# One down projection over all tokens, with seven products made of seven each, in a convolution and SwiGLU layer

## The chip, the cores and the metric

The kernel runs on one core of a Trainium2 chip. The metric is device time in microseconds. PE is TensorE, PEld its weight loads, DVE is VectorE, ACT is ScalarE, POOL is GpSimd and SP is SyncE; SP and ACT issue all DMAs here.

## What is computed

One layer (D = 1024, 2048 tokens, float32): a short gated convolution and a SwiGLU feed-forward, each between two RMS norms with shift, scale and gate that come from a conditioning vector `c`.

```python
mod = silu(c) @ ada_w + ada_b
sh_m, sc_m, g_m, sh_f, sc_f, g_f = split(mod, 6)
h = rms_norm(x, gain0) * (1 + sc_m) + sh_m
b, cc, v = split(h @ conv_w_in, 3)            # 1024 x 3072
h = (b * causal_conv3(cc * v)) @ conv_w_out   # 1024 x 1024
x = x + g_m * rms_norm(h, gain1)
h = rms_norm(x, gain2) * (1 + sc_f) + sh_f
g, u = split(h @ w_gate_up, 2)                # 1024 x 5632
h = (silu(g) * u) @ w_down                    # 2816 x 1024
out = x + g_f * rms_norm(h, gain3)
```

## The kernel before

**Tiling.** Features lie on the 128 partitions, tokens along the rows. The tokens go in two units (u = 0, 1) of 1024, each of two halves of 512 (tok = 0, 1; `CH` = 512). One matmul multiplies a 128 x 128 weight tile by a 128 x 512 tile of features.

**Three matmuls for a product.** Operands are split: `high` (or `upper`) is a cast on ScalarE to the type that TensorE takes in one pass (fp32r), `low` (or `lower`) is the rest, subtracted by VectorE. A product is high x high + low x high + high x low, so a slot of the schedule, four tiles of depth, is 12 matmuls.

**Seven products instead of eight.** Each matrix product of a unit is cut in two along tokens, depth and columns, and done by the Strassen-Winograd scheme with products P1 to P7. The sums of weight blocks and of feature blocks (A11, A12, A22, S1 to S4, see `FEATURES`) are made ahead, stored to HBM and loaded again. The products accumulate in PSUM or are added by VectorE on the way out (`Group.after`).

**Stages.** in0, out0, in1, out1, gu0, down0, gu1, down1 (in: first projection; out: `conv_w_out`; gu: gate and up; down: `w_down`). For a down stage `lockstep` gives an order of slots: seven products, each for four column groups, in three pieces of depth (`SUBS`: 4, 4 and 3 tiles of the 11). Between stages the first two slots of the next are put ahead of the last two of the one before.

**The order of the work is written out by hand.** The main loop walks the slots. `schedule(slot, f)` puts a piece of work at a slot, `later(n, f)` puts it n slots on, a generator's `yield n` waits n slots. Each engine does its instructions in the order of the program. `supply` keeps the weights ahead: loaded 9 slots before use (`BLOCKS`), `high` 5, `low` 4.

**Side work that the change touches.**
- `sums_later("down", ...)`: during gu0 POOL makes the weight sums of both down stages, SP loads the blocks, ACT stores the results.
- `add_square`: the squares of a finished tile (ACT) are added to a running sum, by POOL (`E=G`) except in parts of the last stage.
- `after_out`: norm after the convolution, residual, x1 to HBM, squares for the next norm. For unit 1 it runs in gu0.
- `normalized`: scales, shifts and splits the inputs of a stage at slots around its start; for gu1 this falls at the end of down0.
- `after_down`: norm of a finished half (`norm_of_sums`, `root` on POOL, `diagonal`, `spread`), then eight tiles of output. For unit 0 the halves are stored (`z2_d`) and finished during gu1.
- `last_half`: the last half of the last stage. Its x1 tiles are ready (`before_last`); the last tile's squares go to TensorE at once; output tiles are added on TensorE, POOL and VectorE (`ON_PE`, `ON_POOL`, `LAST_TURN`).

Pools: `raw` 16 tiles of 128 x 512, `big` 17 of 128 x 2048, `tmp` 10, PSUM 8 banks.

## Time and profile before

| | us |
|---|---|
| median of 3 runs (1958.24 to 1961.13) | 1959.97 |
| the profiled execution | 1961.33 |
| its span in the trace | 1959.5 |
| TensorE busy in the span | 1934.8 |
| VectorE busy | 1446.5 |
| ScalarE busy | 899.6 |
| POOL busy | 343.8 |

462.14 MB moved by DMA, 236 GB/s over the span. The granted TensorE clock was 0.998. In the profile L78 is the line of the helper that records every instruction, so groups are told apart by the names of their tiles: `down1P` is a PSUM bank of the stage down1 as well as, with numbers before the P (`down6P`), the weights of a product; `down1S`, `down1A` are features, `down1z` results, `down1q` squares, `o10` the norm of unit 1's first half. A number in the `x` column counts instructions; "idle before" is the engine's idle time just ahead of the group, with what ended it.

### The profile page before, as it was taken

What the parts mean: (1) busy time and instruction counts of PE and PEld (TensorE: products, weight loads), DVE (VectorE), ACT (ScalarE), POOL (GpSimd) and SP (SyncE); (2) the same over time, 40 slices, a digit from 0 to 9 for tenths busy, and PEclk for the clock granted to TensorE, in tenths of its full rate; (3) what the DMA queues carried; (4) which work ended last, traced back from release to release, by engine and by line L of the source; (5) the groups of instructions that cost most, each with busy time, mean ns of one, the idle gap of its engine ahead of it and who ended that gap; (6) DMA issues with size and microseconds to landing.
All of it is one profiled execution on the core that took longest, in us unless ns stands there. A gap on an engine that the chain in (4) does not pass through costs nothing.

```text
span 1959.5 us, 24903 instructions
## 1 busy us (share of the span) xinstructions
PE 1934.8 (99%) x8454; PEld 1570.0 (80%) x8454; DVE 1446.5 (74%) x2069; ACT 899.6 (46%) x1419; POOL 343.8 (18%) x226
## 2 busy tenths in 40 slices
PE   8899999999999999999999999999999999999998
PEld 4678887878878888888888888888888888888886
DVE  4898898977998776997776755587776655665466
ACT  4543457634446743543333454473333333444452
POOL 0012112211221301243341410120100100111011
PEclk9999999999999999999999999999999999999999
DMA  9369979769996764777665977588654332386534
GB/s 390 138 227 373 339 253 349 268 225 371 323 324 216 279 232 149 238 241 244 213 214 183 313 281 269 192 287 279 203 192 140 127 137 97 118 321 226 196 134 133
DMA packets 207632, 462.14 MB, mean 236 GB/s; under 512 B 24465, under 2 KB 39953, under 8 KB 201105
## 3 DMA queue, kind: packets, MB, share of 16 engines
q1 hardware_dynamic: 181584, 406.40, 60.1%
q10 hardware_dynamic: 25920, 54.16, 7.3%
q8 instruction: 66, 1.08, 0.2%
q14 instruction: 62, 0.50, 0.1%
HBM read 329.38 MB, written 131.09 MB: 235 GB/s over the span
## 4 chain that ended last, share of the span: by engine, by line
PE 80%; DVE 8%; DMA 6%; ACT 3%; issue 2%; SPq 0%; ACTq 0%; POOL 0%; DVEq 0%
PE gu1P L78 21%; PE gu0P L78 18%; PE in0P L78 11%; PE down0P L78 11%; PE down1P L78 11%; PE in1P L78 3%; PE out1P L78 2%; PE out0P L78 2%; DMA x<-xx 1%; PE pms L78 1%; DMA kgu1P<-gu1P 1%; DVE in1b L78 0%; DVE in1y L78 0%; DVE gu0a L78 0%; DMA xr<-x_d 0%
## 5 line engine op out<-in xcount | busy, mean ns | idle before, releaser
L78 DVE TENSOR_TENSOR gu1a<-gu1P,gu1a 128x512 f32<-128x512 f32 x63 | 43.5, 691 | 108.5 <-PE gu1P L78 108.5
L78 DVE TENSOR_TENSOR gu0a<-gu0P,gu0a 128x512 f32<-128x512 f32 x63 | 43.3, 688 | 71.7 <-PE gu0P L78 68.8
L78 POOL TENSOR_TENSOR gu1a<-gu1a 128x512 f32<-128x512 f32 x11 | 19.0, 1731 | 360.0 <-DVE gu1g11s L78 39.9
L78 ACT COPY gu1a<-gu1P 128x512 f32<-128x512 f32 x42 | 24.7, 589 | 96.1 <-PE gu1P L78 85.0
L78 POOL TENSOR_TENSOR nq<-nq,nq 128x512 f32<-128x512 f32 x28 | 42.8, 1529 | 136.1 <-ACT nq L78 131.4
L78 ACT COPY gu0a<-gu0P 128x512 f32<-128x512 f32 x42 | 24.4, 586 | 82.2 <-PE gu0P L78 81.0
L78 DVE CUSTOM_DVE_ANT_0 ada<-ada,c 128x512 f32<-128x512 f32 x80 | 60.1, 762 | 0.0
L78 ACT COPY gu1g<-gu1P 128x512 f32<-128x512 f32 x24 | 14.1, 588 | 92.8 <-PE gu1P L78 88.0
L78 POOL TENSOR_TENSOR gu0a<-gu0a 128x512 f32<-128x512 f32 x11 | 19.4, 1767 | 170.6 <-ACT gu0a L78 45.3
L78 ACT COPY gu0g<-gu0P 128x512 f32<-128x512 f32 x24 | 14.1, 589 | 74.4 <-PE gu0P L78 71.0
L78 POOL TENSOR_TENSOR down0q<-down0q,down0q 128x512 f32<-128x512 f32 x14 | 21.0, 1502 | 148.1 <-ACT down0q L78 148.1
L78 ACT ACTIVATE nq<-xx 128x512 f32<-128x512 f32 x32 | 37.1, 1159 | 17.0 <-DVE xx L78 17.0
L78 POOL TENSOR_TENSOR down1q<-down1q,down1q 128x512 f32<-128x512 f32 x10 | 16.1, 1612 | 148.6 <-ACT down1q L78 148.5
L78 DVE TENSOR_TENSOR gu1g<-gu1P,gu1g 128x512 f32<-128x512 f32 x24 | 16.6, 691 | 24.4 <-ACT gu1g L78 23.0
L78 DVE TENSOR_TENSOR down2P<-down2P,down2P 128x512 fp32r<-128x512 f32 x14 | 11.2, 801 | 29.0 <-ACT down2P L78 29.0
L78 ACT ACTIVATE gu1a<-gu1a 128x512 f32<-128x512 f32 x42 | 26.6, 633 | 13.1 <-DVE xo L78 6.0
L78 ACT ACTIVATE gu0a<-gu0a 128x512 f32<-128x512 f32 x42 | 26.6, 634 | 7.3 <-DVE gu0a L78 6.1
L78 POOL TENSOR_TENSOR out1q<-out1q,out1q 128x512 f32<-128x512 f32 x14 | 19.9, 1422 | 55.2 <-ACT out1q L78 55.1
L78 POOL TENSOR_TENSOR out0q<-out0q,out0q 128x512 f32<-128x512 f32 x14 | 20.8, 1485 | 46.9 <-ACT out0q L78 29.7
L78 DVE TENSOR_TENSOR gu0g<-gu0P,gu0g 128x512 f32<-128x512 f32 x24 | 16.5, 689 | 14.3 <-ACT gu0g L78 12.9
L78 DVE TENSOR_TENSOR xx<-xx,zz 128x512 f32<-128x512 f32 x32 | 25.1, 784 | 1.1
L78 ACT ACTIVATE down0q<-down0z 128x512 f32<-128x512 f32 x16 | 18.4, 1153 | 14.9 <-DVE down0z L78 14.8
(3139 smaller groups left out, 6715.8 us busy)
## 6 DMA issues: line engine op xcount, KB each, us to landing
ada<-ada_d SPq DMA_DIRECT2D x64, 256.0 KB, 5.3
act0A<-gu0a SPq DMA_DIRECT2D x33, 256.0 KB, 3.5
act1A<-gu1a SPq DMA_DIRECT2D x33, 256.0 KB, 2.6
ada<-ada_d SPq DMA_DIRECT2D x16, 512.0 KB, 9.5
zz<-z SPq DMA_DIRECT2D x32, 256.0 KB, 5.7
xx<-xt_d SPq DMA_DIRECT2D x32, 256.0 KB, 5.5
x<-xx ACTq DMA_DIRECT2D x32, 256.0 KB, 5.4
down0S<-act0S SPq DMA_DIRECT2D x8, 1024.0 KB, 7.3
```

Source lines behind the costliest of these rows:

```text
L78: return tc.keep_in_program_order(f(*args, **kwargs))
```

## The change

- The two down stages become one, `down0`, after gu1 and over all 2048 tokens. The outer seven products halve tokens within a unit (tok), depth and columns; each is made by seven inner products that halve units, ten of the eleven tiles of depth and the columns again. Tile 11 of the depth is added to four of the inner products (`PLAIN`). One inner product is three steps of 12, 12 and 6 or 12 matmuls.
- Weight sums are made in two passes (`outer_sums`, `inner_sums`) by VectorE during gu0 and the start of gu1; a second pass of feature sums (`feature_sums`, 35 jobs of four) by VectorE during gu1 and, for the last part, the down stage. All go through HBM: SP loads, ACT stores.
- Inner products are collected in eight tiles C11 to C22 by additions on VectorE (`evict`).
- `add_square` uses VectorE everywhere.
- Gu1 follows gu0 directly; its inputs are prepared at gu0's end, two slots later against the stage's start than before (`GU1_EARLY`). The last modulation (`mods_later((5,), ...)`) moves from down0 into gu1. The first product of the down stage is not interleaved with gu1's last slots.
- At the end two halves finish close together: (unit 1, tok 0) and (unit 0, tok 0). The output of the first is kept as eight pieces (`ph.tiles`); two are issued inside the wait times of the other's norm (`fill`), the rest behind its output.
- Small shifts in `normalized` (A11 in two parts, S4 one slot later); the weight sums of the out stages are stored two slots after the addition instead of three.

```diff
-SUBS = ((0, 4), (4, 4), (8, 3))
+KQ = FH // 2
+QW = KQ * 2 * P
+PARTS = ((0, 512), (512, 1024), (1024, QW))
...
+X_LOAD, X_HIGH, X_LOW = 6, 4, 3
+GU1_EARLY = 0
+INNER_AT = (8, 74, 89, 104, 119, 162, 186)
+INNER_EVERY = (9, 5, 5, 5, 5, 8, 8)
...
+OUTER_TURN = ("P1", "P6", "P7", "P4", "P5", "P2", "P3")
+INNER_TURN = ("P1", "P7", "P6", "P4", "P5", "P2", "P3")
+EARLY_TURN = ("P1", "P2", "P6", "P7", "P5", "P4", "P3")
+FIRST_OF = {"P1": "11", "P7": "22", "P6": "21", "P3": "12"}
+SECOND_OF = {"P2": "11", "P5": "22", "P4": "21"}
+LAST_OF = {"P2": "11", "P5": "22", "P4": "21", "P3": "12"}
+PLAIN = {"P2": 0, "P3": 0, "P7": 1, "P4": 1}
+RAW_BLOCK = {"P1": 0, "P2": 3, "P3": 2}
...
+    def block_sums(pace, E, load, n, store):
+        b11, b12 = load(0), load(1)
+        yield pace
+        b22 = load(2)
+        yield pace
+        E.tensor_tensor(b11[:, :n], b12[:, :n], b11[:, :n], ALU.subtract)
+        later(2, partial(store, "P5", b11))
+        b21 = load(3)
+        yield pace
+        E.tensor_tensor(b12[:, :n], b22[:, :n], b12[:, :n], ALU.subtract)
+        later(2, partial(store, "P7", b12))
+        yield pace
+        E.tensor_tensor(b22[:, :n], b22[:, :n], b11[:, :n], ALU.subtract)
+        later(2, partial(store, "P6", b22))
+        yield pace
+        E.tensor_tensor(b21[:, :n], b21[:, :n], b22[:, :n], ALU.subtract)
+        later(2, partial(store, "P4", b21))
+        yield pace
...
+    def outer_sums(pace, E):
+        for op in ("P5", "P7", "P6", "P4"):
+            outer_w[op] = [scratch([P, QW], f"kdown{op}{v}") for v in range(4)] + [scratch([P, CH], f"kdown{op}r")]
+        for v in range(5):
+            for c0, c1 in PARTS if v < 4 else ((0, CH),):
+                part = lambda t, c0=c0, c1=c1: t[:, c0:c1]
+                src = [w_down[b, v] if v < 4 else w_rest[b] for b in range(4)]
+                load = lambda b, src=src, part=part, v=v: from_hbm(part(src[b]), f"down{v}b{b}")
+                store = lambda op, t, part=part, v=v, n=c1 - c0: A.dma_start(part(outer_w[op][v]), t[:, :n])
+                yield from block_sums(pace, E, load, c1 - c0, store)
+    def inner_sums(op, c0, c1, pace, E):
+        src = outer_w[op]
+        load = lambda v: from_hbm(src[v][:, c0:c1], f"downq{op}{v}")
+        store = lambda o, t: A.dma_start(inner_w[op, o][:, c0:c1], t[:, : c1 - c0])
+        yield from block_sums(pace, E, load, c1 - c0, store)
...
+    def all_inner_sums(op, first, every, pace, E):
+        for o in ("P5", "P7", "P6", "P4"):
+            inner_w[op, o] = scratch([P, QW], f"qdown{op}{o}")
+        for n, (c0, c1) in enumerate(PARTS):
+            schedule(first + n * every, lambda c0=c0, c1=c1: run(inner_sums(op, c0, c1, pace, E)))
+        schedule(first + len(PARTS) * every - 1, lambda: run(inner_rest(op, E)))
+    def feature_sums(o, m, pace, lag, E):
+        def load(u, k):
+            t = raw(f"x{o}{u}{k}")
+            SP.dma_start(t, act_d[u][o][:, k, :])
+            return t
+        def store(i, t):
+            A.dma_start(inner_d[o][i][:, m, :], t)
+        x21, x22 = load(1, m), load(1, KQ + m)
+        yield pace
+        x11 = load(0, m)
+        yield pace
+        E.tensor_tensor(x22, x21, x22, ALU.add)
+        later(lag, partial(store, "S1", x22))
+        x12 = load(0, KQ + m)
+        yield pace
+        E.tensor_tensor(x21, x11, x21, ALU.subtract)
+        later(lag, partial(store, "S3", x21))
+        yield pace
+        E.tensor_tensor(x11, x22, x11, ALU.subtract)
+        later(lag, partial(store, "S2", x11))
+        yield pace
+        E.tensor_tensor(x12, x12, x11, ALU.subtract)
+        later(lag, partial(store, "S4", x12))
...
+            units = [(k, g) for k in range(KQ) for g in range(2)][4 * part : 4 * part + 4]
+            if part == 2 and i in PLAIN:
+                units += [(KQ, g) for g in range(2)]
+            self.units = units
...
+    def nested(ph):
+        return [Step(ph, op, i, part) for op in OUTER_TURN
+                for i in (EARLY_TURN if op == OUTER_TURN[0] else INNER_TURN) for part in range(len(PARTS))]
...
-    def add_square(acc, key, z, name, E=G, lag=1, in_turn=True):
+    def add_square(acc, key, z, name, E=V, lag=1, in_turn=True):
...
+            sums = any(op == "P1" and i in ("P5", "P6", "P7") and k == KQ - 1 for _, op, i, k in four)
+            ready = 2 if sums else -X_LOAD
+            schedule(first + max(n - X_LOAD, ready), load)
+            schedule(first + max(n - X_HIGH, ready + 1), upper)
+            schedule(first + max(n - X_LOW, ready + 2), lower)
...
-                                       ("gu", 0), ("down", 0), ("gu", 1), ("down", 1))]
+                                       ("gu", 0), ("gu", 1), ("down", 0))]
...
-        if slots and slots[-1].ph.kind in ("in", "gu"):
+        if slots and slots[-1].ph.kind in ("in", "gu") and not ph.last:
...
+        def tile(k, lag):
+            z = ph.z(u, tok, k)
+            V.tensor_tensor(z, z, rb[0], ALU.mult)
+            V.tensor_tensor(xt[k], xt[k], z, ALU.add)
+            later(lag, partial(A.dma_start, out_tile(u, tok, k), xt[k]))
+        if not tok:
+            load(0)
+            load(4)
+            yield 4.5
+            q = at_once(norm_of_sums(ph.acc[u, tok], f"o{u}{tok}"))
+            yield 1
+            dg = diagonal(q, f"o{u}{tok}")
+            yield 1
+            rb[0] = spread(dg, f"o{u}{tok}")
+            ph.tiles = [partial(tile, k, 0.5) for k in range(KD)]
+            return
+        yield 6
+        q = yield from norm_of_sums(ph.acc[u, tok], f"o{u}{tok}")
+        yield from spread_later(q, f"o{u}{tok}", partial(put, rb, 0), 3)
+        if not u:
+            yield 7
         load(0)
-        yield 1
         load(1)
         yield 2
         for k in range(KD):
             if k + 2 < KD:
                 load(k + 2)
-            z, xt = tiles.pop(k)
-            V.scalar_tensor_tensor(z, z, col(mG[1], k), rb[0], ALU.mult, ALU.mult)
-            V.tensor_tensor(xt, xt, z, ALU.add)
-            later(1, partial(A.dma_start, out_tile(u, tok, k), xt))
-            yield 1.5 if ph.last else 2
+            tile(k, 2.5)
+            yield 1.5
+    LAST = (0, 0)
...
+        def fill():
+            if ph.tiles:
+                ph.tiles.pop(0)()
...
+        fill()
         V.tensor_tensor(v, v, ph.st[:, :4], ALU.add)
-        q = at_once(root(v, "last"))
+        steps = root(v, "last")
+        next(steps)
+        fill()
+        q = at_once(steps)
         dg = tmp("lastd")
...
+        while ph.tiles:
+            fill()
...
+        def done(u, tok, k):
+            t = z(u, tok, k)
+            ph.tiles_done[u, tok] += 1
+            n = ph.tiles_done[u, tok]
+            scaled_z = partial(A.activation, t, t, AF.Copy, scale=col(mG[1], k))
+            if (u, tok) == LAST and n == KD:
+                ph.sq = tmp("lastq")
+                A.activation(ph.sq[:, :CH], t, AF.Square)
+                scaled_z()
+            else:
+                late = not tok and n >= KD - 2
+                later(0 if late else 1, partial(add_square, ph.acc, (u, tok), t, f"down0q{u}{tok}{k}",
+                                               V, 1 if tok else 0.5, False))
+                later(1 if late else 2, scaled_z)
+                if (u, tok) == LAST and n == KD - 1:
+                    later(1.5, partial(all_but_one, ph))
+            if n == KD:
+                run(after_down(ph, u, tok))
+        def evict(op, i, g):
+            t = ph.bank[op, i][g]
+            c = FIRST_OF.get(i) or SECOND_OF[i]
+            u, n = int(c[0]) - 1, g + 2 * (int(c[1]) - 1)
+            to, base = {"P1": ("C11", None), "P6": ("C12", "C11"), "P7": ("C22", "C12"), "P4": ("C21", "C22"),
+                        "P5": ("C12", "C12"), "P2": ("C11", "C11"), "P3": ("C12", "C12")}[op]
+            dst = tile_of(to, u, n)
+            if op == "P5" and u:
+                if i in FIRST_OF:
+                    parts[u, n] = tmp(f"down0t{u}{n}")[:, :CH]
+                    A.copy(parts[u, n], t)
+                else:
+                    p = parts[u, n]
+                    V.tensor_tensor(p, t, p, ALU.add)
+                    c22 = tile_of("C22", u, n)
+                    V.tensor_tensor(c22, c22, p, ALU.add)
+                    V.tensor_tensor(dst, dst, p, ALU.add)
+            elif op == "P1" and i in FIRST_OF:
+                A.copy(dst, t)
+            else:
+                V.tensor_tensor(dst, t, tile_of(base, u, n) if base and i in FIRST_OF else dst, ALU.add)
+                if op == "P5":
+                    c22 = tile_of("C22", u, n)
+                    V.tensor_tensor(c22, t, c22, ALU.add)
+            if LAST_OF.get(i) == c and op in ("P2", "P3", "P5", "P4"):
+                tok, up = {"P2": (0, 0), "P3": (0, 1), "P5": (1, 1), "P4": (1, 0)}[op]
+                done(u, tok, n + 4 * up)
+        def product(s, only=None):
+            op, i = s.op, s.i
+            kind = {"P2": "pb", "P7": "pd", "P4": "pd"}.get(i, "pa")
+            if (op, i) not in ph.bank:
+                if i in ("P1", "P2", "P7"):
+                    ph.bank[op, kind] = [bank(f"down0P{op}{kind}_{g}") for g in range(2)]
+                ph.bank[op, i] = ph.bank[op, kind]
+            final = (KQ if i in PLAIN else KQ - 1)
+            for x, (k, g) in enumerate(s.units):
+                if only is not None and g != only:
+                    continue
+                acc = ph.bank[op, i][g]
+                t, j = ph.at[op, i, k] if k < KQ else ph.at[op, "rest", PLAIN[i]]
+                hi, lo = t[1][:, j, :], t[2][:, j, :]
+                c = slice(x * P, (x + 1) * P)
+                wh, wl = s.w.w[:, 0, c].bitcast(F32R), s.w.w[:, 1, c].bitcast(F32R)
+                PE.matmul(acc, wh, hi, start=k == 0 and i in ("P1", "P2", "P7"), stop=False, skip_group_check=True)
+                PE.matmul(acc, wl, hi, start=False, stop=False, skip_group_check=True)
+                PE.matmul(acc, wh, lo, start=False, stop=k == final, skip_group_check=True)
+                if k == final:
+                    evict(op, i, g)
...
-    schedule(first["gu0"] + 64, lambda: run(sums_later("down", range(12), 1.1)))
+    gu0, gu1, down = (first[n] for n in ("gu0", "gu1", "down0"))
+    schedule(gu0 + 4, lambda: run(outer_sums(0.95, V)))
+    for n, op in enumerate(OUTER_TURN):
+        all_inner_sums(op, gu0 + INNER_AT[n], INNER_EVERY[n], 1.25, V)
+    for m in range(KQ):
+        for n, op in enumerate(OUTER_TURN):
+            at = (28 * (m + 1) + 10 + 4 * n, 1.0, 3) if m < KQ - 1 else (149 + 14 * n, 1.0, 3) if n else (149, 0.7, 1.5)
+            schedule(gu1 + at[0], lambda op=op, m=m, at=at: run(feature_sums(FEATURES[op], m, *at[1:], V)))
     schedule(first["out0"] - 2, lambda: run(mods_later((3,), 1.25)))
     schedule(first["out0"] - 23, lambda: run(mods_later((2,), 1.0)))
     schedule(first["in1"] + 60, lambda: run(mods_later((4,), 1.25)))
-    schedule(first["down0"] + 22, lambda: run(mods_later((5,), 2)))
-    schedule(first["down1"] + 73, lambda: before_last(phases[-1]))
+    schedule(gu1 + 4, lambda: run(mods_later((5,), 1.25)))
+    schedule(len(slots) - 2, lambda: before_last(phases[-1]))
...
+        if i >= len(slots) - 3:
+            a, b, c = slots[-3:]
+            for x, g in (((a, 0), (b, 0)), ((c, 0), (a, 1)), ((b, 1), (c, 1)))[i - len(slots) + 3]:
+                s.ph.product(x, g)
+        elif s.ph.last:
+            s.ph.product(s)
+        else:
+            multiply(s)
```

More of the change, by code (lines that the diff above doesn't have):

```diff
@@ L908, in hybrid_conv_layer @@
         ph = s.ph
[L909 removed]
+        if ph.kind == "down":
+            w = Weight(ph.kind, s.part, s.op + s.i, Piece(s.op, s.i, s.part))
+        elif ph.kind == "out":
             w = Weight(ph.kind, s.grp, s.op, None, ks=s.ks)
@@ L1083, in hybrid_conv_layer @@
     for ph in phases:
-        if ph.kind not in ("out", "down"):
+        if ph.kind == "down":
+            inner_products(ph)
+        if ph.kind != "out":
             continue
@@ L1391, in hybrid_conv_layer @@
         if ph.kind in ("out", "down"):
-            loaded(ph, own[ph.name], f)
+            (loaded if ph.kind == "out" else streamed)(ph, own[ph.name], f)
             continue
```

279 lines of the change are left out of this document (168 added, 111 removed).

## Prediction

> **What bounds the kernel now.** I read the page's first two parts, then the chain that ended last in order of time, then the windows by stage.
>
> ```profile
> span 1959.5 us, 24903 instructions
> PE 1934.8 (99%) x8454; PEld 1570.0 (80%) x8454; DVE 1446.5 (74%) x2069; ACT 899.6 (46%) x1419; POOL 343.8 (18%) x226
> ...
> 1093.32 5.44 PE down0P L78 x24
> 1098.76 5.44 PE gu0P L78 x24
> 1104.20 160.49 PE down0P L78 x708
> ...
> 1265.48 43.67 PE down0P L78 x192
> 1309.15 16.32 PE gu1P L78 x72
> ...
> 1326.26 397.29 PE gu1P L78 x1752
> ```
>
> TensorE is the bound. From 1093 us on the chain is an unbroken run of its matmuls, and they pass at one rate: 5.44/24 = 0.2267 us, 397.29/1752 = 0.2268. The first down stage is 24 + 708 + 192 = 924 of them, 209.4 us.
>
> Now the busy time by stage. The first row is in1, then come two of gu0, the first half of down0, two of gu1, two of down1, and the end:
>
> ```profile
> 350.00:590.00 240.00, 236.14 (x1052) 194.29 (x1051) 210.81 (x316) 111.60 (x169) 48.75 (x31) 1.00 0.88 308
> ...
> 671.00:880.00 209.00, 208.32 (x927) 172.45 (x926) 170.65 (x214) 100.12 (x155) 52.79 (x33) 1.00 0.66 219
> 880.00:1093.00 213.00, 212.39 (x941) 175.50 (x940) 157.06 (x196) 78.12 (x136) 76.09 (x50) 1.00 0.65 215
> 1093.00:1200.00 107.00, 107.00 (x474) 88.63 (x473) 65.99 (x83) 52.82 (x71) 20.69 (x13) 1.00 0.87 315
> ...
> 1309.00:1520.00 211.00, 211.00 (x936) 174.85 (x935) 153.44 (x215) 81.85 (x136) 18.39 (x12) 1.00 0.63 210
> 1520.00:1729.00 209.00, 209.00 (x923) 173.06 (x923) 127.27 (x186) 77.33 (x133) 19.71 (x12) 1.00 0.39 135
> 1729.00:1830.00 101.00, 101.00 (x447) 83.62 (x447) 54.47 (x62) 45.88 (x64) 9.68 (x5) 1.00 0.71 249
> 1830.00:1941.00 111.00, 110.94 (x496) 91.48 (x495) 65.73 (x78) 50.97 (x74) 11.81 (x8) 1.00 0.47 157
> 1941.00:1959.50 18.50, 11.64 (x39) 5.22 (x37) 8.05 (x17) 3.69 (x6) 3.56 (x3) 0.93 0.35 114
> ```
>
> The columns after the length are busy us of PE, PEld, DVE, ACT and POOL, the granted clock, the share of the DMA engines, and GB/s. VectorE is 78% busy in gu0 (327.7 of 422), 67% in gu1 (280.7 of 420) and 57% in the last down stage (120.2 of 212). That idle time is what the change spends.
>
> **The matmuls.** Before, a down stage is 7 products x 4 column groups x 11 tiles of depth x 3 matmuls = 924, twice 1848. After, each of the seven outer products is seven inner ones of 5 tiles x 2 groups x 3 = 30, and four of these carry 6 more for the eleventh tile: 7 x (210 + 24) = 1638. So 210 go: 210 x 0.2267 = **-47.6 us**, all on the path. The norms cost TensorE a little too:
>
> ```profile
> 1264.69 0.78 PE o00s L78 x8
> ...
> 1898.55 0.86 PE o10b L78 x2
> ...
> 1935.52 1.05 PE lasts L78 x8
> ```
>
> Before: sums of squares for three halves (0.78 each), one row spread by TensorE (0.86), and the last half's 1.05 with half a microsecond of wait, 4.8 us. After: three halves with sums and spread, 4.9, and the same 1.05 and wait, 6.5: **+1.7**.
>
> **What one VectorE instruction costs.** The groups by line of the last down stage, and the timeline:
>
> ```profile
> L78 DVE TENSOR_TENSOR down1z<-down1P,down1z 128x512 f32<-128x512 f32 x11 | 7.6, 688 | 8.0 <-PE down1P L78 8.0
> ...
> L78 DVE TENSOR_TENSOR down1S<-down1S,down1S10h 128x2048 fp32r<-128x2048 f32 x1 | 2.3, 2293 | 1.3 <-ACT down1S10h L78 1.3
> ```
>
> ```profile
> 702.27 2.29 DVE L78 TENSOR_TENSOR gu0S1l<-gu0c,gu0S1h 128x2048 fp32r<-128x2048 f32 x1
> 704.48 2.28 DVE L78 TENSOR_TENSOR gu0b<-gu0b,gu0a 128x2048 f32<-128x2048 f32 x1
> ...
> 1819.86 0.69 DVE L78 TENSOR_TENSOR down4P<-down4P,down4P 128x512 fp32r<-128x512 f32 x1
> 1820.46 0.69 DVE L78 TENSOR_TENSOR down5P<-down5P,down5P 128x512 fp32r<-128x512 f32 x1
> ```
>
> One lasts 0.69 us, but the next starts 0.60 us after it (2.21 for 2048 columns). The slope, 1.045 ns a column, makes 0.34 for 256.
>
> **VectorE in the new last stage** (371.3 us of matmuls). Low halves of the weights: 49 products x 3 pieces, 126 x 0.605 + 21 x 0.34 = 83. Low halves of the features: 245 tiles in fours, 61 x 2.21 + 0.6, and 14 single, 8.5: 144. Evictions: two a product, but each tile of P5 goes to two or three places, and eight are ScalarE's copies at P1 and four at P5: 100 x 0.61 = 61. Squares 27 x 0.605 = 16. Output of two of the four norms, 16 tiles x (0.72 + 0.61, the add waits for the product) = 21. Six of the 35 feature sums still to do, 24 x 0.605 = 15. Norms and leftovers 6. Sum 346, 93%. Work can be done only three or four steps (8 to 10 us) ahead, so the spread counts: an outer product has 53.0 us; its fixed part is 32.4, evictions make it 41 (P1 36), and in P2 squares and ten output tiles make about 58. That lag of 5 us is within the lead. I take **+4** here, between 0 (an even spread) and 22 (the first rival).
>
> By the Trainium skill, "VectorE: DVE Perf Modes", section "The TRN2 errata", an fp32 add of N columns takes (N+151)/0.96 ns, 691 at 512 and 2291 at 2048. Its durations agree with the rows; whether the next instruction waits for the whole of one is what the starts above decide, and they say no. If it had to wait out each one, the stage would go the first rival's way.
>
> **VectorE and POOL in the gate-and-up stages.**
>
> ```profile
> L78 DVE TENSOR_TENSOR gu9P<-gu9b,gu9P 128x512 fp32r<-128x512 f32 x7 | 8.1, 1160 | 0.0
> ...
> L78 DVE TENSOR_TENSOR gu5P<-gu5b,gu5P 128x512 fp32r<-128x512 f32 x7 | 4.8, 684 | 0.0
> ...
> L78 POOL TENSOR_TENSOR nq<-nq,nq 128x512 f32<-128x512 f32 x14 | 21.9, 1565 | 58.9 <-ACT nq L78 54.3 <-DMA down1b<-w_down_d 4.6
> ...
> L78 POOL TENSOR_TENSOR down4b<-down4b,down4b 128x512 f32<-128x512 f32 x4 | 6.0, 1497 | 9.3 <-DMA down4b<-w_down_d 9.3
> ```
>
> The same subtraction costs 684 ns with POOL idle and 1160 beside POOL's adds (first two rows, gu0). Less what each does for another stage's residual (some 32 instructions, 20 us), gu0 has 307 us of VectorE and gu1 260, with 129 and 38 us of POOL: about half a microsecond of VectorE per microsecond of POOL. The squares (0.6 on VectorE for 1.5 on POOL) are therefore free: **0**, bounds -4 and +4 in in1, where VectorE is at 88% without the path minding.
>
> Gu0: outer sums 36 x 0.605 + 16 x 0.34 = 27, five of the inner sums at 6.5 = 33, squares 11, less 45 for POOL: 354 of 422, 84%. Gu1: outputs -20, feature sums 116 x 0.605 = 70, two inner sums 13, the last modulation's 16 at 0.7, 11: 354 of 420, 84%. The first window ran at 88% and lost TensorE 4 us in 240 (1.6%); gu0 at 78% lost under 1 us in each half. 1.6% of 842 would be 13, none 0; I take **+4**. It falls at gu0's end, where gu1's inputs are now prepared beside gu0's own tail instead of beside the down stage; if that cover fails, first late is the low half of gu1's first features.
>
> **DMA.** The last stage moves 259 feature tiles (67.9 MB), weights 35.8, the rest of the sums 12.6, x1 and 16 output tiles 12.6: 129 MB, less 4 loaded ahead, 337 GB/s; gu0 rises from 217 to about 275, gu1 from 173 to about 318. Another window:
>
> ```profile
> 441.00:490.00 49.00, 48.48 (x213) 39.55 (x212) 38.70 (x61) 22.01 (x33) 7.34 (x5) 1.00 1.02 371
> ```
>
> 371 GB/s, with TensorE idle 0.5 us. So it fits, just: **0**, upper bound below. ScalarE and SP:
>
> ```profile
> L78 ACT CAST down7P<-down7P 128x512 fp32r<-128x512 f32 x7 | 4.3, 621 | 6.4 <-PE down1P L78 4.3 <-PE gu1P L78 2.1
> ...
> L78 ACT CAST down1S11h<-down1S 128x2048 fp32r<-128x2048 f32 x1 | 1.9, 1915 | 0.0
> ```
>
> ```profile
> 1800.92 0.33 SPq L78 DMA_DIRECT2D down2P<-w_down_d  x1
> ```
>
> ScalarE has 61 casts of features (117 us), 147 of weights (91) and some 90 other instructions of about 0.6, 262 of 371; SP issues some 350 DMAs (116 us). Neither binds.
>
> **The end.**
>
> ```profile
> 1944.32 1.02 POOL L78 TENSOR_TENSOR lastq<-lastv,mhalf 128x4 f32<-128x4 f32 x1 [29.24 <-DVE lastv L78]
> ...
> 1946.91 0.69 DVE L78 TENSOR_TENSOR down1z<-down1z,lastb 128x512 f32<-128x512 f32 x1 [0.66 <-PE lastb L78]
> ...
> 1947.63 0.69 DVE L78 TENSOR_TENSOR xl<-xl,down1z 128x512 f32<-128x512 f32 x1
> 1948.24 4.27 DVE L78 TENSOR_TENSOR down1z<-down1z,lastb 128x512 f32<-128x512 f32 x7
> ...
> 1952.55 0.69 DVE L78 TENSOR_TENSOR xl<-xl,down1z 128x512 f32<-128x512 f32 x1
> ...
> 1953.94 0.34 ACTq L78 DMA_DIRECT2D out_d<-xl  x1
> ```
>
> Before, one half's output ran under matmuls and eight tiles stood behind them. Now sixteen do: two are filled into VectorE's waits for TensorE's sums and for POOL's root (the second may delay the root by some 0.4 us), six come after VectorE's last add at 1952.55: 6 x 1.33 = 8.0. ScalarE's issues end at 1953.94, so the last one moves to about 1961.5; it then goes alone, not behind seven others, which gives back about 1. **+6.5**, bounds +4 and +9.
>
> **Sum** against the profiled execution's 1961.33 (span 1959.5): 1961.3 - 47.6 + 1.7 + 4 + 4 + 6.5 = 1929.9. The median of the runs is 1.4 below that execution: **1928**. I call 0.2% (4 us) what a measurement of this kernel can tell.
>
> **Rivals.**
> - VectorE becomes the bound of the last stage (0.20). If each instruction held VectorE for its whole duration (0.69, 2.29), the same counts make 375 us, and the outer products P4, P5, P2, P3 need 54, 58, 63 and 58 where TensorE has 53 each: 21 late, less a lead of 7 at best, 15 to 22 more: 1943 to 1950. For it: 93% by the cheap count. Against: the 0.60 us starts.
> - DMA binds (0.08). In the first half of down0 315 GB/s took 87% of the engines; if about 315 were all that this mix gives, 125 MB take 397 us: 26 more, 1950. Against: 371 above.
> - Slower (0.07). VectorE now does in its own order what POOL did: each job of four sums waits for loads. POOL stood 9.3 us in the down4b row. There are 69 such jobs (13 outer, 21 inner, 35 feature). VectorE has 68 us idle in gu0 and 66 in gu1; with the 32 us of gain, waits of over 166 / 69 = 2.4 us a job use up everything. At 3 us, 69 x 3 - 166 = 41 beyond that, about 2000. Against: POOL was early at its adds, and VectorE comes in its turn, two steps of their pace after the load (0.95 to 1.25 slots of 12 matmuls each: 5.2 to 6.8 us).
> - The change does not do what it says (0.03): 210 matmuls shorter, but other stalls of 28 to 36 us, near 1960.
>
> The forecast holds 0.62. Its own range is 1916 (no stall, the end at +4, a few microseconds won where POOL no longer shuts out VectorE) to 1938. The range, 1914 to 1951, takes in the first two rivals. Faster 0.90, same 0.03, slower 0.07.
>
> **What would show it.** Right: 1638 products in the last stage at 0.2267 us, TensorE over 98% in gu0 and gu1, VectorE some 85% there and over 90% in the last stage, 25 us from the last product to the end. Wrong: TensorE waiting for VectorE's low halves from P5 on (first rival), for feature loads (second), VectorE waiting for DMA in the sums (third).

## The result and the profile after

The changed kernel takes 1934.47 us (median of 4 runs, 1932.94 to 1943.3) against 1959.11 us for the kernel before beside it (1957.38 to 1961.13): a ratio of 0.9883 [0.9851, 0.9915]. Faster, as forecast, and inside the range, but the median lies 6.5 us above the forecast 1928. The profiled execution took 1932.94 us, with a span of 1931.2.

First the busy times and the DMA volume on the page of the changed kernel:

```profile
span 1931.2 us, 25610 instructions
PE 1891.2 (98%) x8248; PEld 1528.0 (79%) x8248; DVE 1649.7 (85%) x2529; ACT 935.1 (48%) x1438; POOL 154.4 (8%) x98
...
DMA packets 280359, 589.10 MB, mean 305 GB/s; under 512 B 32288, under 2 KB 58528, under 8 KB 273952
```

TensorE lost 43.6 us of busy time and still bounds the kernel. VectorE rose from 74 to 85%, POOL halved, and 127 MB more went by DMA. (L94 is now the line of the recording helper.)

The windows of the changed kernel, with the columns of before: two for gu0, two for gu1, then the seven outer products P1, P6, P7, P4, P5, P2, P3 of the last stage:

```profile
671.00:880.00 209.00, 206.78 (x913) 169.27 (x911) 185.89 (x285) 98.23 (x151) 21.63 (x11) 1.00 0.95 326
880.00:1095.00 215.00, 213.45 (x941) 175.74 (x942) 170.30 (x271) 85.56 (x150) 20.84 (x13) 1.00 0.76 258
1095.00:1306.00 211.00, 211.00 (x933) 174.71 (x932) 182.03 (x288) 81.27 (x138) 18.10 (x10) 1.00 0.93 323
1306.00:1513.00 207.00, 207.00 (x915) 171.41 (x914) 174.19 (x262) 74.75 (x132) 20.32 (x12) 1.00 0.93 318
...
1521.00:1576.00 55.00, 54.39 (x237) 43.83 (x236) 43.77 (x47) 33.79 (x41) 2.98 (x2) 1.00 1.03 388
1576.00:1629.00 53.00, 53.00 (x236) 43.88 (x235) 45.55 (x52) 31.38 (x36) 0.00 (x0) 1.00 0.99 378
1629.00:1682.00 53.00, 53.00 (x236) 43.88 (x235) 44.82 (x51) 29.69 (x32) 0.00 (x0) 1.00 0.95 346
1682.00:1735.00 53.00, 53.00 (x236) 43.88 (x235) 48.59 (x58) 36.42 (x44) 0.00 (x0) 1.00 0.95 338
1735.00:1789.00 54.00, 54.00 (x244) 44.87 (x243) 48.33 (x59) 36.27 (x50) 0.00 (x0) 1.00 0.85 304
...
1846.30:1905.70 59.40, 55.15 (x244) 44.51 (x243) 56.90 (x76) 36.08 (x48) 1.51 (x1) 1.00 0.83 304
```

Read DVE (the third busy time) against the length. Gu0 and gu1 hold 356 us of VectorE each; gu1 loses TensorE nothing, gu0 4 us. P6, P7 and P4 take their bare 53.0 us, but in P3 (last row) VectorE is busy 56.90 of 59.40 us and TensorE idle 4.2. These are the waits that the view by engine names, in gu0 and in the last stage:

```profile
PE gu0P L94 <- ACT gu0a L94: 3.5, 5, 1.0
...
PE down0PP3pa L94 <- DVE down0x L94: 2.7, 1, 2.7
PE down0PP3pd L94 <- DVE down0x L94: 1.5, 1, 1.5
```

(us in total, times, longest.) `down0x` is the low half of the features: in P3 TensorE waits for VectorE's subtractions. In gu0 the row names ScalarE, which empties a PSUM bank too late; ScalarE itself, from 815 to 900 us, waits longest for VectorE's additions of the residual, which stand ahead in its order:

```profile
ACT nq L94 <- DVE xx L94: 10.7, 9, 2.0
```

The chain of waits shows that the rate of the matmuls did not change, 6.80/30 = 0.2267 us:

```profile
1106.83 399.74 PE gu1P L94 x1764
...
1629.05 6.80 PE down0PP7pa L94 x30
1635.85 8.16 PE down0PP7pd L94 x36
```

From the first matmul of gu0 to the last product took 1941.3 - 674.8 = 1266.5 us before and 1905.7 - 672.7 = 1233.0 after. All stages of the traces, in us (from the first matmul of a stage to that of the next; "end" is from the last product):

| kernel | to gu0 | gu0 | gu1 | P1 | P6 to P5 | P2 | P3 | end | median of runs | ratio to before |
|---|---|---|---|---|---|---|---|---|---|---|
| before | 674.8 | 418.5 | | | | | | 18.2 | 1959.11 | |
| changed | 672.7 | 423.1 | 425.3 | 54.8 | 213.0 | 57.4 | 59.4 | 25.5 | 1934.47 | 0.9883 [0.9851, 0.9915] |
| e8 (the same again) | 674.2 | 422.3 | 425.7 | 56.1 | 213.1 | 57.4 | 59.4 | 25.4 | 1936.05 | 0.9889 [0.9869, 0.9909] |
| e1 | 675.6 | 422.7 | 425.4 | 56.3 | 213.1 | 57.4 | 61.9 | 25.5 | 1938.39 | 0.9889 [0.9874, 0.9903] |
| e2 | 674.0 | 424.1 | 425.4 | 56.9 | 213.1 | 56.2 | 53.9 | 25.5 | 1930.26 | 0.9848 [0.9833, 0.9862] |
| e3 | 674.6 | 428.4 | 425.4 | 56.8 | 213.0 | 57.4 | 59.5 | 25.4 | 1944.84 | 0.9922 [0.9907, 0.9937] |
| e5 | 676.9 | 424.3 | 426.1 | 55.0 | 213.1 | 57.4 | 60.7 | 25.5 | 1940.74 | 0.9901 [0.9886, 0.9916] |
| e6 | 672.7 | 423.5 | 426.0 | 57.5 | 213.1 | 57.3 | 59.5 | 19.9 | 1930.1 | 0.9849 [0.9834, 0.9863] |
| e7 | 677.3 | 426.6 | 425.3 | 56.2 | 213.1 | 57.4 | 60.7 | 25.4 | 1942.58 | 0.9915 [0.9898, 0.9932] |
| e9 | 675.8 | 424.1 | 425.3 | 54.4 | 213.0 | 57.4 | 60.7 | 26.0 | 1937.85 | 0.9887 [0.9872, 0.9902] |
| e10 | 677.3 | 423.4 | 425.3 | 53.8 | 213.1 | 57.6 | 59.0 | 26.0 | 1938.08 | 0.9887 [0.9870, 0.9904] |
| e11 | 676.0 | 418.0 | 436.2 | 55.2 | 213.0 | 57.4 | 60.7 | 25.5 | 1943.55 | 0.9920 [0.9905, 0.9934] |
| e12 | 674.5 | 418.9 | 437.5 | 56.8 | 213.1 | 57.7 | 58.9 | 26.1 | 1942.71 | 0.9913 [0.9896, 0.9931] |

The runs of one kernel differ by some microseconds (why is shown further down), so a question about one stage is answered from its column, not from the medians.

### The profile page after: what moved, and what is told of

Read it like the earlier page. It is cut to its first block, busy times and chain, and to the rows that moved or that the text cites. A ratio compares the mean times of both kernels' runs of the same rounds, so it can differ in the third digit from the quotient of the medians.

```text
span 1931.2 us, 25610 instructions
## 1 busy us (share of the span) xinstructions
PE 1891.2 (98%) x8248; PEld 1528.0 (79%) x8248; DVE 1649.7 (85%) x2529; ACT 935.1 (48%) x1438; POOL 154.4 (8%) x98
## 4 chain that ended last, share of the span: by engine, by line
PE 73%; DMA 14%; DVE 8%; ACT 2%; issue 2%; SPq 0%; POOL 0%; ACTq 0%; DVEq 0%; POOLq 0%
PE gu1P L94 21%; PE gu0P L94 17%; PE in0P L94 11%; PE in1P L94 8%; PE out1P L94 4%; DVE down0zC L94 2%; PE down0PP4pa L94 1%; PE down0PP7pa L94 1%; PE down0PP6pa L94 1%; DMA out_d<-down0xo 1%; PE out0P L94 1%; DVE down0x L94 1%; DMA ada<-ada_d 1%; PE down0PP4pd L94 1%; PE down0PP7pd L94 1%
## 5 line engine op out<-in xcount | busy, mean ns | idle before, releaser
L94 DVE TENSOR_TENSOR gu0a<-gu0P,gu0a 128x512 f32<-128x512 f32 x63 | 43.3, 687 | 38.4 <-PE gu0P L94 37.1
L94 DVE TENSOR_TENSOR gu1a<-gu1P,gu1a 128x512 f32<-128x512 f32 x63 | 43.3, 687 | 36.2 <-PE gu1P L94 36.1
L94 DVE TENSOR_TENSOR xS<-xS,xS 128x512 f32<-128x512 f32 x80 | 62.5, 781 | 5.8 <-DMA xS<-act0S 4.6
L94 ACT COPY gu1a<-gu1P 128x512 f32<-128x512 f32 x42 | 24.6, 586 | 81.2 <-PE gu1P L94 75.8
L94 DVE CUSTOM_DVE_ANT_0 ada<-ada,c 128x512 f32<-128x512 f32 x80 | 58.9, 748 | 0.0
L94 ACT COPY gu0a<-gu0P 128x512 f32<-128x512 f32 x42 | 24.5, 586 | 68.8 <-PE gu0P L94 60.2
L94 ACT COPY gu1g<-gu1P 128x512 f32<-128x512 f32 x24 | 14.1, 589 | 83.3 <-PE gu1P L94 75.0
L94 DVE TENSOR_TENSOR downqP<-downqP,downqP 128x512 f32<-128x512 f32 (+1 forms) x84 | 53.3, 634 | 0.0
L94 DVE TENSOR_TENSOR xA<-xA,xA 128x512 f32<-128x512 f32 x60 | 41.1, 685 | 8.1 <-DMA xA<-act0A 4.6
L94 POOL TENSOR_TENSOR gu1a<-gu1a 128x512 f32<-128x512 f32 x11 | 19.0, 1728 | 356.7 <-DVE gu1g11s L94 39.6
L94 POOL TENSOR_TENSOR gu0a<-gu0a 128x512 f32<-128x512 f32 x11 | 18.8, 1710 | 347.1 <-DMA kdownP<-down3b 67.0
L94 ACT ACTIVATE nq<-xx 128x512 f32<-128x512 f32 x32 | 37.1, 1158 | 13.0 <-DVE xx L94 12.8
L94 ACT COPY gu0g<-gu0P 128x512 f32<-128x512 f32 x24 | 14.1, 593 | 58.9 <-PE gu0P L94 54.1
L94 ACT ACTIVATE gu1a<-gu1a 128x512 f32<-128x512 f32 x42 | 26.6, 633 | 19.4 <-DVE gu1a L94 9.1
L94 ACT ACTIVATE gu0a<-gu0a 128x512 f32<-128x512 f32 x42 | 26.6, 633 | 15.4 <-DVE gu0a L94 10.5
L94 ACT ACTIVATE down0q<-down0zC 128x512 f32<-128x512 f32 x31 | 19.2, 632 | 26.9 <-DVE down0zC L94 26.7
L94 ACT ACTIVATE out0q<-out0z 128x512 f32<-128x512 f32 x16 | 18.4, 1151 | 15.2 <-DVE out0z L94 15.0
L94 ACT ACTIVATE out1q<-out1z 128x512 f32<-128x512 f32 x16 | 18.4, 1148 | 14.3 <-DVE out1z L94 14.1
L94 DVE TENSOR_TENSOR xx<-xx,zz 128x512 f32<-128x512 f32 x32 | 22.1, 692 | 1.5 <-DMA xx<-xt_d 0.4
L94 ACT ACTIVATE xr<-xr 128x512 f32<-128x512 f32 (+1 forms) x24 | 18.5, 771 | 9.8 <-DMA xr<-x_d 9.7
L94 ACT ACTIVATE down0zC<-down0zC,mG 128x512 f32<-128x512 f32 x32 | 21.6, 715 | 1.2 <-DMA out_d<-down0xo 0.8
L94 POOL TENSOR_TENSOR o11q<-o11v,mhalf 128x4 f32<-128x4 f32 x1 | 1.0, 1007 | 253.9 <-DVE o11v L94 253.9
```

The source lines that it names most:

```text
L94: return tc.keep_in_program_order(f(*args, **kwargs))
```

## The experiments

### The changed kernel again (e8)

No edit; it gives the stages a second time, beside other runs.

> The changed kernel itself, unedited, beside the others on the same chip: 1932 to 1938, with the outer products and stages within 1 us of those of its first trace at the same granted clock.

It measured 1936.05 us (1935.31 to 1943.15). P2, P3 and the end come back within 0.1 us, gu0 within 0.8, P1 only within 1.3.

### How much the matmuls alone are worth (e4)

```diff
 # kernel before
-            PE.matmul(acc, wl, hi[:, k, :], start=False, stop=False, ...)
+            if not (s.ph.kind == "down" and s.sub == 1 and (s.n, k) != (3, 3)):
+                PE.matmul(acc, wl, hi[:, k, :], start=False, stop=False, ...)
```

> The kernel before with 105 matmuls left out of each down stage (low weights x high features in the middle piece of depth, for 15 of its 16 tiles), 210 in all, and nothing else. If every matmul is on the path at 0.2267 us: 47.6 us faster, 1912. If something behind them takes their place (weights, features or the end), less than 40.

Measured: 1916.36 us (1916.01 to 1917.78) against 1961.04, a ratio of 0.9778 [0.9762, 0.9795]: 44.7 us won where 47.6 of matmuls go. The term stands. In the traces the two down stages give 46.3 of the 47.6 us, the last one with a wait of 1.4 for VectorE's `down1q` near its end; gu1 takes 1.9 us longer than before, with a wait of 1.6 for `gu1a`. So what the changed kernel misses beyond these few microseconds lies in what the change adds.

### Why P2 and P3 are late: the queue of loads, or VectorE (e1, e5, e2)

In the changed kernel SyncE's queue waits long for output stores in this stretch, and so it does in e5 (first row changed, second e5):

```profile
SPq L94 <- DMA out_d<-down0xo: 35.2, 9, 9.2
```

```profile
SPq L94 <- DMA out_d<-down0zC: 38.9, 7, 8.7
```

Theory A reads from it that the output tiles hold buffers, the queue stops behind them, and the feature loads come late. Theory B is that VectorE has too much to do. E1 takes the output tiles from another pool, e5 does not load x1 for them at all, e2 leaves out a part of VectorE's work.

```diff
 # e1
-                xt[k] = tmp(f"down0xo{u}{tok}{k}")[:, :CH]
+                xt[k] = raw(f"down0xo{u}{tok}{k}")
 # e5
-                xt[k] = tmp(f"down0xo{u}{tok}{k}")[:, :CH]
-                SP.dma_start(xt[k], x1_d[u][tok][:, k, :])
+                xt[k] = ph.z(u, tok, k)
 # e2
-            V.tensor_tensor(z, z, rb[0], ALU.mult)
+            if not tok:
+                V.tensor_tensor(z, z, rb[0], ALU.mult)
```

> The changed kernel with one edit: the x1 tiles of the two tok-1 output halves are loaded into the raw pool instead of tmp. VectorE's work and the bytes moved stay the same. Theory A (SP's queue: it stands 35 us in all on tmp tiles whose output DMA has not landed, and weights and features stand behind it): SP's waits for out_d<-down0xo go away, the outer products P2 and P3 (57.4 and 59.3 us, where 53.0 is the matmuls' own) come down to about 55 and 54, and the kernel is about 6 us faster than the changed one, 1927. Theory B (VectorE is full there, 52.5 of 53 us): P2 and P3 keep their length within 1 us, 1933.

> The changed kernel without the loads of x1 for the two tok-1 output halves: the second instruction of each of those sixteen tiles adds the tile to itself, and the tile goes out from where it lies, so that they put out twice the scaled z. VectorE does as many instructions as in the changed kernel; there is no load for SP to stand on, no buffer that an output DMA holds, and 4.2 MB less are moved. Theory A (SP's queue): P2 and P3, from P2's first product to the last one 116.8 us in the changed kernel, come down to about 110. Theory B (VectorE is full; the edit without the multiplication brought 110.1 there with SP still waiting 23 us): they stay within 2 us of 116.8.

> The changed kernel without the multiplication by the norm in the sixteen tok-1 output tiles (they put out x1 plus the unnormalized z). It takes 16 x 0.66 = 10.6 us of VectorE out of P2 and P3, and leaves buffers, queues and DMAs as they are. Theory B: P2 and P3 go down to about 55 and 55, 6 us faster than the changed kernel, 1927. Theory A: SP still stands on the output tiles, at most 2 us faster, 1931 to 1933.

E1 did not take the wait away (37.5 us remained), so it says nothing against A; its P3 is 2.5 us longer, at a granted clock of 0.94. In e5 the loads and their buffers are gone, but the queue's row stays under the name of another tile, so e5 alone takes away the cause that A names and not the wait; P2 and P3 are no shorter. The windows of P2 and P3 in e5, then in e2:

```profile
1795.40:1852.80 57.40, 56.67 (x248) 45.37 (x247) 56.71 (x81) 36.99 (x48) 2.01 (x2) 1.00 0.78 271
1852.80:1913.50 60.70, 56.42 (x243) 45.69 (x242) 56.89 (x76) 35.94 (x48) 1.51 (x1) 0.97 0.68 239
```

```profile
1793.50:1849.70 56.20, 56.04 (x248) 45.48 (x247) 55.21 (x77) 40.52 (x52) 2.02 (x2) 1.00 0.82 293
1849.70:1903.60 53.90, 53.90 (x243) 44.81 (x242) 47.74 (x64) 32.49 (x44) 1.40 (x1) 1.00 0.89 330
```

In e5 the DMA engines are busy 0.68 of P3 instead of 0.83, and VectorE still 56.89 us: P3 is 60.7 long, 1.3 more than in the changed kernel, where the granted clock was 1.00 instead of 0.97. With 16 multiplications less (e2) VectorE has 9 us less work in P3 and 6 to spare, TensorE never waits there (53.90 of 53.90), and the two products take 110.1 us instead of 116.8. What VectorE itself waits for in the changed kernel, from 1790 to 1905 us, is this and no more:

```profile
DVE down0q L94 <- ACT down0q L94: 0.7, 1, 0.7
DVE o10d L94 <- POOL o10q L94: 0.3, 1, 0.3
```

It never stands for a load or a feature tile. Theory B holds: VectorE's work is the bound here, for 6.7 us. The 35 us row of the queue was no cause: in e2 it still shows 23.0 us, and TensorE waits for nothing in P3. SyncE runs ahead, and such a row only names what happened last.

### Squares on POOL again (e3)

```diff
-    def add_square(acc, key, z, name, E=V, lag=1, in_turn=True):
+    def add_square(acc, key, z, name, E=G, lag=1, in_turn=True):
```

> The changed kernel with the sums of squares of the out stages and of the residual back on POOL; the last stage's stay on VectorE. By the forecast this part costs nothing either way: within 4 us of the changed kernel, 1930 to 1937. If the 2.8 us that TensorE loses in gu0 from 860 to 900 us come from too much on VectorE (95 to 97% busy there), it is 2 to 3 us faster than the changed one; if POOL's additions hold VectorE up there by more than they save it, gu0 gets longer than its 423.0 us.

Gu0 takes 428.4 us instead of 423.1 (422.3 in e8). The windows up to 815 us and of the residual of unit 1 (815 to 900), first the changed kernel, then e3:

```profile
671.00:815.00 144.00, 143.34 (x633) 117.65 (x632) 123.52 (x187) 66.81 (x105) 14.65 (x7) 1.00 0.94 327
815.00:900.00 85.00, 81.89 (x362) 66.05 (x362) 80.53 (x128) 39.95 (x61) 10.58 (x6) 1.00 0.92 307
```

```profile
671.00:815.00 144.00, 140.31 (x617) 114.23 (x616) 123.39 (x179) 67.76 (x106) 23.39 (x13) 1.00 0.93 320
815.00:900.00 85.00, 79.53 (x351) 64.61 (x350) 83.68 (x112) 38.95 (x60) 26.02 (x17) 1.00 0.94 317
```

In the two stretches 17 additions move to POOL, which is busy 24 us more. On VectorE they were worth 17 x 0.605 = 10.3 us, but it is busy 3.0 us more without them, 83.68 of 85 in the second stretch, and TensorE loses 5.4 us more. So 24 us of POOL cost VectorE at least 13, a little over the half that the forecast reckoned with. (VectorE does 24 instructions fewer in the two stretches, not 17; if the other seven are worth 0.605 us each as well, an estimate from the same figure, it is 17.5.)

How POOL does it shows in the profile of before, in the seven `gu9P` subtractions whose mean of 1160 ns the forecast used: four took 0.68 us, and three 1.79 to 1.81. Each of the three began just after an addition of POOL and ended 0.55 us after it:

```profile
860.54 1.69 POOL L78 TENSOR_TENSOR nq<-nq,nq 128x512 f32<-128x512 f32 x1
861.00 1.79 DVE L78 TENSOR_TENSOR gu9P<-gu9b,gu9P 128x512 fp32r<-128x512 f32 x1
```

The Trainium skill ("SBUF — State Buffer", section "Who interferes with whom") says that a VectorE instruction with two inputs in SBUF shuts out a POOL instruction that reads SBUF, and the other way round, whichever comes first; the three long rows agree. So having the squares on VectorE, costed at nothing, is worth 5 to 6 us here.

The rest of gu0's loss lies in 815 to 900, where residual, outer weight sums and gu0's own evictions fall together. The busy share alone does not tell it. In the same stretch of before VectorE was busier, with fewer but longer instructions, and TensorE lost 0.6 us:

```profile
815.00:900.00 85.00, 84.39 (x380) 69.63 (x379) 84.31 (x98) 41.63 (x64) 40.09 (x26) 1.00 0.80 254
```

### Can gu0's loss be moved away (e7, e11)

```diff
 # e7: the residual of unit 1 slower
-            yield 2
+            yield 3 if u else 2
...
 # e11: the outer sums rest while the residual passes
-INNER_AT = (8, 74, 89, 104, 119, 162, 186)
-INNER_EVERY = (9, 5, 5, 5, 5, 8, 8)
+INNER_AT = (8, 108, 120, 132, 164, 178, 192)
+INNER_EVERY = (9, 4, 4, 4, 5, 5, 5)
...
+            if v == 3:
+                yield 24
```

> The changed kernel with unit 1's residual after the convolution (zz, xx, squares, in gu0) at three slots a tile instead of two, its second half eight slots later so that the halves don't overlap. The work is the same. If gu0's lost microseconds come from VectorE being full from 815 to 900 us (80.5 of 85), TensorE gets back about 2 of its 3.1 idle us there, and gu0 falls from 423.0 to about 421. If they come from the outer sums' waits for loads, or from ScalarE's queue, gu0 keeps its length within 1 us.

> The changed kernel with the outer sums of the weights stopped while the residual of the unit before passes in the first gate-and-up stage (24 slots, about 150 us further on), and the inner sums moved later for it. Theory (the 4.5 us of this stage are lost where residual and outer sums stand together, at 815 to 900 us, where TensorE now loses 3.1): the stage takes 419 to 420 us instead of 423, the time 1933. Rival (VectorE's work is only moved, and its slack in this stage is used up wherever it falls, as when the residual was moved): the loss appears later in the stage, 423 to 427, the time 1936 to 1940.

(E7 also starts the residual of the unit's second half eight slots later.) Nothing is lost from 815 to 900 us, but 6.4 us right behind. The residual's end meets the inner sums there, and VectorE stands 3.9 us for the load of one of their blocks; that this meeting costs the 6.4 us is read off the times and was not tried:

```profile
815.00:900.00 85.00, 85.00 (x381) 70.49 (x380) 77.33 (x122) 39.65 (x61) 11.50 (x7) 1.00 0.91 305
900.00:930.00 30.00, 23.64 (x99) 18.84 (x98) 22.77 (x36) 9.28 (x15) 1.42 (x1) 0.96 0.97 335
```

In e11 TensorE is busy all 85 us from 815 to 900, and gu0 comes down to 418.0 us, as the theory of the collision had it. But the sums then fall into gu1, which takes 436.2 us instead of 425.3, and the kernel is slower. Its window of that loss, and then its waits in gu1:

```profile
1230.00:1300.00 70.00, 62.30 (x262) 49.75 (x262) 58.85 (x93) 21.92 (x39) 7.11 (x4) 0.98 0.98 338
```

```profile
PE gu1P L94 <- DVE gu7P L94: 2.6, 2, 1.4
...
PE gu1P L94 <- DVE gu8P L94: 2.5, 1, 2.5
...
DVE xS L94 <- DMA xS<-act1S: 6.2, 2, 3.2
DVE xS L94 <- DMA xS<-act0S: 5.2, 3, 3.2
```

VectorE is idle 11 of these 70 us, and TensorE still waits: 8.4 us in all of gu1, 5.1 of them for VectorE and 3.3 for ScalarE, where it waited 0.7 in the changed kernel. (One of these waits is followed by 3.4 us at half clock, 1.7 us more.) VectorE stands before an addition whose load has not come (up to 3.2 us at a time, the DMA engines 0.98 busy), with the low halves of the weights `gu7P` and `gu8P` queued behind it. That is the mechanism of the forecast's slower rival, and it comes true as soon as sums stand closer together. Part of the rival theory of e11 holds too: the later places that it used were not free.

### The end (e6, e9)

```diff
 # e6: the eight tiles of the other half left out
-            ph.tiles = [partial(tile, k, 0.5) for k in range(KD)]
+            ph.tiles = []
 # e9: another order of the last six tiles
-        while ph.tiles:
-            fill()
+        for k in on_pe:                    # two of the six: x by TensorE
+            add_on_pe(k, 0)
+        for k in rest:
+            scale(k)                       # multiplication, VectorE
+            if k in on_pe:
+                add_on_pe(k, 1)            # z by TensorE, copy by ScalarE
+        for k in rest[2:]:
+            add(k, 0.5)                    # addition, VectorE
```

> The changed kernel without the eight output tiles of the half (unit 1, tok 0), which are not written. The prediction put them at 6.5 us behind the last product: then the time from the last product's sums of squares to the span's end falls from 25.5 us to about 18.5, and nothing else moves. If the two tiles filled into the waits also hold up the root and the diagonal, it falls below 18.2, the length before.

> The changed kernel with another order of its last six output tiles: all six multiplications first, two of the six additions made by TensorE in a free bank and copied by ScalarE, the other four on VectorE behind the multiplications. Theory (after the last product VectorE's queue is the path, six tiles of two instructions): two additions and the pause between each multiplication and its addition go, 2 x 0.61 + 6 x 0.11 = 1.9 us; the tail from the last product to the end goes from 25.5 to about 23.5 and the time from 1936 to 1934; nothing else in the trace moves. Rival (the end hangs on the output stores that ScalarE issues, not on VectorE): the tail stays at 25.5, or grows, since ScalarE now copies two tiles before it issues.

Without the eight tiles the end takes 19.9 us instead of 25.5: they cost 5.6. The other 1.7 against before's 18.2 show in the timelines of TensorE: the sums of the last tile's squares start 1909.2 - 1905.7 = 3.5 us after the last product, where before they started 1943.0 - 1941.3 = 1.7 after it. In e6 it is 3.5 too. What stands ahead of them on TensorE since the change are the sums of the other squares (0.95) and the spread of the other half's norm (1.10). E9 ends VectorE's work earlier and wins nothing. VectorE's last instructions in the timeline and a window of the end with the DMA engines' share, first of the changed kernel (last product at 1905.7), then of e9 (1910.7):

```profile
1926.26 0.69 DVE L94 TENSOR_TENSOR down0zC<-down0zC,o10r 128x512 f32<-128x512 f32 x1
1926.98 0.69 DVE L94 TENSOR_TENSOR down0xo<-down0xo,down0zC 128x512 f32<-128x512 f32 x1
```

```profile
1918.00:1930.00 12.00, 1.52 (x4) 0.30 (x2) 9.43 (x15) 1.52 (x3) 1.15 (x1) 0.74 0.98 328
```

```profile
1928.20 2.48 DVE L94 TENSOR_TENSOR down0xo<-down0xo,down0zC 128x512 f32<-128x512 f32 x4
```

```profile
1923.00:1935.00 12.00, 4.92 (x12) 1.82 (x10) 7.65 (x13) 2.66 (x5) 1.11 (x1) 0.89 1.01 326
```

VectorE ends 1927.67 - 1905.7 = 22.0 us after the last product in the one and 1930.68 - 1910.7 = 20.0 in the other; the kernel ends after 25.5 and 26.0. For 12 us the DMA engines are full (0.98, 1.01): sixteen output tiles of 256 KB are 4.2 MB, at 328 GB/s 12.8 us. The rival holds: with two halves at the end the output stores set it. ScalarE's last issues, first of the changed kernel, then of e9:

```profile
1920.83 7.21 ACTq L94 DMA_DIRECT2D out_d<-down0xo  x8
```

```profile
1928.71 3.57 ACTq L94 DMA_DIRECT2D out_d<-down0xo  x7
```

They end 1928.0 - 1905.7 = 22.3 us after the last product in the one and 1932.3 - 1910.7 = 21.6 in the other. So in e9 the issuing ended earlier too and the kernel did not: the transfers end last there. In the changed kernel VectorE's last addition (22.0), the last issue and the full DMA engines lie so close together that the trace does not part them.

### Output tiles in pairs, and all edits together (e10, e12)

```diff
-        for k in range(KD):
+        for k in range(0, KD, 2):
...
-            tile(k, 2.5)
-            yield 1.5
+            scale(k)
+            scale(k + 1)
+            add(k, 2.5)
+            add(k + 1, 2.5)
+            yield 3
```

> The edit of the end as in the run before, and the output tiles of the second token half in the last stage made in pairs (two multiplications, then two additions, then a rest as long as before), so that no addition follows the product it needs at once. Theory that VectorE is full in outer products P2 and P3, where 52.5 of 53 us are busy: 16 pauses of 0.11 us go, 1.8 us over the two, which take 115 instead of 116.8; with the end 1932. Rival (VectorE is late there for what it waits for, not for its own work): 116.8 stays and the time is that of the run before.

> The three edits of the runs before in one kernel. If each of them takes from a wait of its own, their gains add: 1.9 at the end, 1.8 in P2 and P3 and 3 in the first gate-and-up stage, about 1929. If the pause of the outer sums only moves the loss, 1932 or more.

E10 stands beside e9, whose granted clock in P3 was 0.97 as well: P2 and P3 take 116.6 us instead of 118.1, so 1.5 of the 1.8 expected. The pauses between dependent instructions were part of VectorE's load. In the median, 1938.08 against 1937.85, the gain does not show. E12 repeats each part at its place (gu0 418.9, gu1 437.5, P2 and P3 116.6, end 26.1) and is slower than the changed kernel by e11's loss. No version that still computes the whole layer has a lower median than the changed kernel's 1934 to 1936 us.

## Why the prediction was right, and where it was off

Against the profiled execution, by its own steps:

| term | forecast | measured |
|---|---|---|
| matmuls | -47.6 | -47.6 counted at the same rate; -44.7 alone (e4) |
| norms' small matmuls | +1.7 | 3.3 - 3.8 = -0.5 up to the last product, the rest is in the end |
| last stage | +4 | 381.2 - 371.3 = 9.9, before 1.0: +8.9 |
| gu0 and gu1 | +4 | 426.0 + 419.9, before 421.3 + 419.0: +5.5 |
| squares | 0 | left on POOL they would have cost 5 to 6 (e3) |
| end | +6.5 | 25.5 - 18.2 = +7.3 |
| stages up to gu0 | 0 | -2.1 |

(The stages are sums, over both traces, of the times from the start of each matmul to the start of the next. Before's two down stages took 419.9 us, 1.0 over the 418.9 of their matmuls alone.) The sum was 1929.9; the profile says 1932.9. The direction and the main term were right, and the range held. That the sum came within 3 us is in part luck: the last stage, gu0 with gu1 and the end were 7.2 us too low, and two terms that went the other way, -2.1 up to gu0 and 2.2 less for the norms, gave 4.3 back.

**Last stage: the step "that lag of 5 us is within the lead".** P2's own load was sized about rightly (58 forecast with ten output tiles, 56.7 busy of 57.4 with eight). P3 was put behind it as if it had room to catch up, but the other eight output tiles and ten additions of squares fall there. By the forecast's own prices that is 41 + 8 x 1.33 + 10 x 0.605 = 57.7, and VectorE is busy 56.9 us in it. So P2's lag is not worked off, it grows: 4.2 us of idle TensorE in P3. The rival that VectorE becomes the bound was half right: the place and the order (P2, then P3), but not P4 and P5, which stayed at 53.1 and 53.9, and not by whole durations. E2's 6.7 us is its size, not 15 to 22.

**Gu0 and gu1: nearly the right sum of two wrong terms.** With the squares left on POOL the two stages would have come to about +11 (5.5 and e3's 5 to 6), not to the same sum. "The squares are therefore free" set 0.6 us against three quarters and called it nothing; in gu0's crowded stretches this difference is TensorE's. The new sums were counted as an even 84% (356 of 424 us came of it), and the loss was put at gu0's end. It came at 815 to 900 us, where three kinds of work fall into one stretch; from 900 us to gu0's end TensorE lost nothing.

**The end: "it then goes alone".** The forecast was 7.5 for six tiles behind VectorE's last add, less 1 for a store without seven others beside it. The tiles cost 5.6 and the new order 1.7, and the last store does not go alone: the DMA engines are full for 12 us. VectorE's rows gave about the right size by a chain that, shortened by 2 us in e9, did not shorten the end: luck.

**DMA.** As the bound of the whole stage it fell: the stage ran at up to 388 GB/s with a busy share of 1.03 (P1), and e5's lower share made P3 no shorter. P1, 54.8 to 57.5 us instead of 53.0, is the stretch where the DMA engines are fullest, and there the sign of the second rival does show. TensorE waits for low halves of features (`down0x`), VectorE for ScalarE's high halves, and ScalarE for the tiles' loads, in P1 of the changed kernel:

```profile
DVE down0x L94 <- ACT down0x20h L94: 2.6, 1, 2.6
...
ACT down0x20h L94 <- DMA down0x<-fA11S: 3.2, 1, 3.2
```

So the forecast's 0 for DMA misses about 2 to 4 us in P1. Whether these loads are late because the engines are full or because they are issued late was not tried.

**The stages up to gu0.** Most of the -2.1 is the chance of one execution. The changed kernel's trace and e6's have no stretch at half clock ahead of gu0 and start it at 672.7 us; the other twelve traces, that of before among them, have two or more and start it at 674.0 to 677.3. E8, the changed kernel again, has the same two as before and starts gu0 at 674.2, 0.6 us before it. The last section shows such stretches.

**From the profiled execution to the median.** The forecast took the 1.4 us by which before's median lies under its profile off the sum as well. After, the profiled execution is the fastest of four, and the median lies 1.5 above it. With the 3.0 us of the sum and a rounding of half a microsecond this makes the 6.5.

## What to carry to other kernels

- An average load says little once work comes in bursts: add up each stretch of about the length of the lead, and carry the lag of one into the next, which may have no room either.
- A wait row with large numbers on an engine that runs ahead (35 us on a DMA queue) is a symptom until its removal moves the bound. Read first what the late engine itself waits for (VectorE: for no load), then take its work away (e2).
- Adding work to an engine of 85% means that a piece moved out of one crowd lands in the next (e7, e11): leave it unless the place it goes to is known to be free. The share alone does not say whether it is: 84.31 of 85 us cost TensorE 0.6 before, 80.53 cost it 3.1 after.
